# A feed-forward kernel with all five full chunks in seven block products, on ScalarE and VectorE queues written out by hand

## The chip, the cores and the metric

The kernel runs on one NeuronCore of one Trainium2 chip. The metric is the device time of one execution in microseconds (us), the median over the runs shown. TensorE (PE) multiplies matrices into PSUM, VectorE (DVE) and ScalarE (ACT) work elementwise on SBUF and PSUM, GpSimd (POOL) does small work and issues the adding transfers, SyncE (SP) issues the loads.

## The reference, cut to what matters

A trunk of four layers over 256 tokens of width 1024, all in float32. Each layer is a feed-forward block, an attention block (one of three kinds) and a second feed-forward block, so there are eight feed-forward blocks, and only they are changed:

```python
D_FF = 2816
def swiglu(x, w_in, w_out):
    gate, up = jnp.split(x @ w_in, 2, axis=-1)
    return (jax.nn.silu(gate) * up) @ w_out
...
h = h + 0.5 * rms_norm(swiglu(rms_norm(h, g[0]), ffn_w_in[i, 0], ffn_w_out[i, 0]), g[1])
```

## The kernel before, in words

**Precision.** Every product is made of three float32r matmuls: an operand is split into a rounded part `hi` and a rest `lo` (`hilo`, L155 to L157: a copy on ScalarE makes `hi`, then a subtraction on VectorE makes `lo`), and hi·hi, lo·hi and hi·lo are added up in PSUM (`product`, L139). Splitting the weights is most of the work of ScalarE and VectorE.

**Chunks.** A feed-forward block (`ffn`, L282) walks over the 2816 hidden columns in six chunks: five of 512 columns and one of 256. Before, the narrow one stands second: chunk 0 full, chunk 1 narrow, chunks 2 to 5 full. A chunk multiplies both 128-token tiles (t = 0 and 1) by its gate and up weights, applies SiLU and the product, turns the result on TensorE (`turn`) and multiplies it by its rows of `w_out` (`out`), which is done one chunk later (`o(t, k)` inside the next chunk).

**Plain and Winograd chunks.** A chunk in `plain` makes eight block products (two token tiles, two halves of the depth, gate and up) of 12 matmuls each. A full chunk listed in `WINO` goes through `wino` and makes seven, a Strassen-Winograd scheme: the weight quarters are b00, b01 (upper half of the depth, gate and up) and b10, b11 (lower half), and the sums t1 = b00 + b01, t3 = b01 + b11, t2 = t1 + b11 = b00 + t3 and t4 = t2 + b10 (the signs are in the activations and in `nr`). Of these four sums two are additions on VectorE (L372, 128x2048 each) and two are transfers that add while they write, issued by GpSimd (L375). Each of the seven weights is then split.

**Buffers.** A loaded or summed weight lies in one of `RAWS = 9` raw buffers; its split pair lies in one of `UNITS = 4` slots, which `close` frees after the product that reads it. `fill()` issues whatever loads and splits (`preps`, in a fixed order) have room, so the split of unit n + 4 is issued right after the product of unit n. The units of a Winograd chunk are used in the order b00, b10, t2, o0, t1, t3, b11, o2, t4, where o0 and o2 are the two pieces of the chunk before in `w_out`.

**Order of the queues.** A tile framework schedules the traced program: it keeps dependencies, simulates the engines with a cost model, and sorts each engine's instructions by readiness and by the order in which they were written. So the order on ScalarE and VectorE before is the scheduler's. A call of `keep_in_program_order` pins an instruction behind the one traced just before it on the same engine. Once compiled, each engine's list is fixed.

**Where a chunk ends.** After product t4 the gate of tile 1 is closed: VectorE adds (L482), ScalarE applies SiLU (L518), VectorE multiplies (`up`, L426). The next chunk copies its first product to SBUF on ScalarE (`sl0`, L487) before product t2 may be added to the same PSUM bank.

## Time and profile before

| | us |
|---|---|
| median of 3 runs (2003.55 to 2004.16) | 2004.0 |
| profiled execution: its own time | 2004.23 |
| profiled execution: span of the profile | 2002.3 |
| TensorE busy in the span | 1932.5 (97%) |
| VectorE busy | 1609.4 (80%) |
| ScalarE busy | 1257.2 (63%) |

The span runs from the first to the last instruction; 1.9 us of the execution's time lie outside it. Shares are averages over stages that have different limits, so the feed-forward blocks are read by themselves below. The granted TensorE clock was 1.00 (the 2.4 GHz level) in every stretch shown. L numbers are lines of the kernel before.

### The profile page before, as it was taken

Reading aid. Unit: us, or ns where it says so; the run is one execution under the profiler, and the core shown is the slowest. Engines: PE = TensorE matmul, PEld = TensorE weight load, DVE = VectorE, ACT = ScalarE, POOL = GpSimd, SP = SyncE. Lnnn points to the kernel's source line nnn. Section 1 sums busy time; section 2 is a strip of 40 time slices with the busy share of each in tenths; the row PEclk is TensorE's granted clock in tenths of the full one; section 3 lists DMA queues with packets and bytes.
Section 4 is the critical chain, followed back from the end, with each engine's and each line's share of the span. In section 5 each row is a group of like instructions: output and inputs, shape, how many; then the busy total and the mean of one; then the engine's idle time right before and its main releaser. Section 6 shows DMA issues by size and latency. Waiting matters only on the chain.

```text
span 2002.3 us, 25733 instructions
## 1 busy us (share of the span) xinstructions
PE 1932.5 (97%) x9712; PEld 1584.9 (79%) x9712; DVE 1609.4 (80%) x2040; ACT 1257.2 (63%) x1721; POOL 188.6 (9%) x303
## 2 busy tenths in 40 slices
PE   7999999999999999999999999999999999999998
PEld 6777878777877878877887787678778777878776
DVE  6888678888788766788879877877988888678886
ACT  6566666566566566566656666865666657576654
POOL 0001210000000120000000032000000000210000
PEclk9999999999999999999999999999999999999999
DMA  9795638696787556687877675166868785638782
GB/s 360 213 295 140 211 120 294 184 294 188 245 274 222 169 189 212 184 278 211 283 221 212 209 205 165 60 242 200 230 208 300 202 286 148 206 105 286 203 286 55
DMA packets 177867, 430.25 MB, mean 215 GB/s; under 512 B 8784, under 2 KB 37712, under 8 KB 169552
## 3 DMA queue, kind: packets, MB, share of 16 engines
q1 hardware_dynamic: 168528, 361.51, 50.7%
q0 software_dynamic: 9216, 67.11, 17.6%
q8 instruction: 76, 1.25, 0.2%
q14 instruction: 47, 0.39, 0.1%
HBM read 360.43 MB, written 1.05 MB: 181 GB/s over the span
## 4 chain that ended last, share of the span: by engine, by line
PE 79%; ACT 8%; DVE 7%; issue 3%; POOL 0%; ACTq 0%; DVEq 0%; POOLq 0%
PE ps L152 13%; PE pb L152 12%; PE y L246 9%; PE y L244 9%; PE y L245 9%; PE pc L152 6%; ACT hi L156 5%; PE pa L152 4%; PE pw L670 4%; PE pw L672 4%; PE pw L671 3%; DVE lo L157 3%; DVE raw L372 2%; PE tpg L434 1%; ACT gh L156 1%
## 5 line engine op out<-in xcount | busy, mean ns | idle before, releaser
L157 DVE TENSOR_TENSOR lo<-raw,hi 128x2048 fp32r<-128x2048 f32 (+3 forms) x534 | 984.7, 1861 | 251.3 <-ACT hi L156 250.8
L156 ACT CAST hi<-raw 128x2048 fp32r<-128x2048 f32 (+3 forms) x534 | 824.8, 1563 | 481.6 <-DVE raw L372 189.9
L244 PE MATMUL y<-hi,gh 128*128 128x512 f32 x704 | 277.6, 394 | 5.1 <-ACT gh L156 5.1
L245 PE MATMUL y<-lo,gh 128*128 128x512 f32 x704 | 275.2, 391 | 0.0
L246 PE MATMUL y<-hi,gl 128*128 128x512 f32 x704 | 265.7, 391 | 0.0
L152 PE MATMUL ps<-hi,xh 128*128 128x256 f32 (+1 forms) x512 | 175.4, 342 | 1.9 <-ACT xh L156 1.3
L152 PE MATMUL pb<-hi,sh 128*128 128x512 f32 x384 | 153.1, 399 | 21.1 <-ACT sl L487 21.1
L152 PE MATMUL ps<-lo,xh 128*128 128x256 f32 (+1 forms) x512 | 173.2, 338 | 0.2 <-DVE lo L157 0.2
L152 PE MATMUL ps<-hi,xl 128*128 128x256 f32 (+1 forms) x512 | 172.9, 338 | 0.0
L244 PEld LDWEIGHTS y<-hi,gh 128*128 128x128 f32 x704 | 132.2, 188 | 41.7 <-ACT gh L156 15.2
L670 PE MATMUL pw<-hi,xh 128*128 128x512 f32 (+2 forms) x432 | 164.6, 381 | 0.0
L672 PE MATMUL pw<-hi,xl 128*128 128x512 f32 (+2 forms) x432 | 155.9, 361 | 0.0
L671 PE MATMUL pw<-lo,xh 128*128 128x512 f32 (+2 forms) x432 | 155.4, 360 | 0.0
L246 PEld LDWEIGHTS y<-hi,gl 128*128 128x128 f32 x704 | 132.2, 188 | 27.4
L375 POOL DMA_DIRECT2D raw<-raw x64 | 55.5, 868 | 1037.6 <-DVE raw L372 644.3
L245 PEld LDWEIGHTS y<-lo,gh 128*128 128x128 f32 x704 | 132.3, 188 | 26.0
L152 PE MATMUL pb<-lo,sh 128*128 128x512 f32 x384 | 151.8, 395 | 0.0
L152 PE MATMUL pb<-hi,sl 128*128 128x512 f32 x384 | 149.5, 389 | 0.0
L372 DVE TENSOR_TENSOR raw<-raw,raw 128x2048 f32<-128x2048 f32 x64 | 146.0, 2282 | 0.0
L152 PEld LDWEIGHTS ps<-hi,xh 128*128 128x128 f32 x512 | 97.6, 191 | 13.2 <-ACT xh L156 2.2
L152 PEld LDWEIGHTS pb<-hi,sh 128*128 128x128 f32 x384 | 72.0, 188 | 45.3 <-ACT sl L487 31.2
L152 PEld LDWEIGHTS ps<-lo,xh 128*128 128x128 f32 x512 | 97.6, 191 | 11.2 <-DVE lo L157 1.1
(213 smaller groups left out, 3327.2 us busy)
## 6 DMA issues: line engine op xcount, KB each, us to landing
raw<-in_ffn_w_in SPq DMA_DIRECT2D x172, 1024.0 KB, 8.4
raw<-in_ffn_w_out SPq DMA_DIRECT2D x88, 1024.0 KB, 9.2
raw<-raw POOLq DMA_DIRECT2D x64, 1024.0 KB, 7.0
raw<-in_diff_w_in SPq DMA_DIRECT2D x24, 1024.0 KB, 5.2
raw<-in_moba_w_in SPq DMA_DIRECT2D x12, 1024.0 KB, 5.2
raw<-in_nsa_w_in SPq DMA_DIRECT2D x9, 1024.0 KB, 5.1
raw<-in_diff_w_out SPq DMA_DIRECT2D x8, 1024.0 KB, 4.9
gpre<-in_norm_g SPq DMA_DIRECT2D x12, 512.0 KB, 5.9
```

Of the source, the lines that this page charges most:

```text
L152: nc.tensor.matmul(out, l, r, start=first and i == 0, stop=last and i == len(steps) - 1, skip_group_check=more)
L156: self.nc.scalar.copy(hi, src)
L157: self.nc.vector.tensor_tensor(lo, src, hi.bitcast(F32), op=ALU.subtract)
L244: nc.tensor.matmul(y[b], x[0][:, kt, :], hi[:, k, s], start=f, stop=False)
L245: nc.tensor.matmul(y[b], x[0][:, kt, :], lo[:, k, s], start=False, stop=False)
L246: nc.tensor.matmul(y[b], x[1][:, kt, :], hi[:, k, s], start=False, stop=l)
L372: nc.vector.tensor_tensor(R[name(to)], R[name(a)], R[name(b)], op=ALU.add)
L375: nc.gpsimd.dma_start(R[name(to)], R[name(b)], accum_op=ALU.add)
L434: nc.tensor.transpose(tp[:, k, :], g[:, k * P:(k + 1) * P], self.ident)
L670: nc.tensor.matmul(out, x[0][:, kt, :], hi[:, k, :], start=first and i == 0, stop=False)
L671: nc.tensor.matmul(out, x[0][:, kt, :], lo[:, k, :], start=False, stop=False)
L672: nc.tensor.matmul(out, x[1][:, kt, :], hi[:, k, :], start=False, stop=last and i == len(todo) - 1)
```

## The change

- The narrow chunk becomes chunk 0, and all five full chunks (1 to 5) become Winograd chunks.
- The sums of a chunk's weights are ordered otherwise: t1 goes into a raw buffer of its own and t3 = b01 + b11 is added by transfer; both are issued one chunk ahead (`sums_of(j + 1)`, after the first output products of chunk j). t2 = b00 + t3 follows on VectorE when b10 is split, t4 = t2 + b10 by transfer when t2 is split.
- The gate of tile 1 (`gate1`) moves from the end of its chunk to behind the first product and the `sl0` copy of the next, and the `fill()` that stood at the chunk's end goes.
- Inside `wino` every instruction of ScalarE and VectorE is pinned in the order in which it is written (`placed`); TensorE is not.
- The first product of chunk 1 is put in the middle of the narrow chunk, ahead of the turning of tile 1's activations and of their sums (`begin`).

```diff
-WINO = (2, 3, 4, 5)
+WINO = (1, 2, 3, 4, 5)
...
     def hilo(self, src, hi, lo):
-        self.nc.scalar.copy(hi, src)
-        self.nc.vector.tensor_tensor(lo, src, hi.bitcast(F32), op=ALU.subtract)
+        self.placed(self.nc.scalar.copy(hi, src))
+        self.placed(self.nc.vector.tensor_tensor(lo, src, hi.bitcast(F32), op=ALU.subtract))
+    def placed(self, ins):
+        return self.tc.keep_in_program_order(ins) if self.ordered else ins
...
-            chunks.insert(1, (D_FF - 256, 256))
+            chunks.insert(0, (D_FF - 256, 256))
...
             def plan_wino(j):
                 c0, w = chunks[j]
                 name = lambda n: (j, n)
                 quarter = lambda k, u: (w_in, k * 512, 4, u * D_FF + c0, w)
                 c1, w1 = chunks[j - 1]
                 ko = [((j - 1, "o", k), (w_out, c1 + k * P, 2, 0, D)) for k in range(0, w1 // P, 2)]
-                for n, src in ((name("b00"), quarter(0, 0)), (name("b01"), quarter(0, 1)),
-                               (name("b10"), quarter(1, 0)), (name("b11"), quarter(1, 1)), (name("t2"), None), *ko):
+                for n, src in ((name("b00"), quarter(0, 0)), (name("b01"), quarter(0, 1)), (name("b11"), quarter(1, 1)),
+                               (name("t1"), None), (name("b10"), quarter(1, 0)), *ko):
                     loads.append(lambda n=n, src=src: raw(n, src))
-                def add(to, a, b):
-                    nc.vector.tensor_tensor(R[name(to)], R[name(a)], R[name(b)], op=ALU.add)
-                def add_by_dma(to, b):
-                    nc.gpsimd.dma_start(R[name(to)], R[name(b)], accum_op=ALU.add)
-                def quarters(n, then=()):
-                    split(name(n), name(n))
-                    for x in then:
-                        (add if len(x) == 3 else add_by_dma)(*x)
-                def last_of(n, of, gone=None):
-                    split(name(n), name(of), True)
-                    if gone:
-                        free(name(gone))
+                def sum_t2():
+                    split(name("b10"), name("b10"))
+                    self.placed(nc.vector.tensor_tensor(R[name("b00")], R[name("b00")], R[name("b01")], op=ALU.add))
+                def split_t2():
+                    split(name("t2"), name("b00"))
+                    nc.gpsimd.dma_start(R[name("b00")], R[name("b10")], accum_op=ALU.add)
+                def split_t4():
+                    split(name("t4"), name("b00"), True)
+                    free(name("b10"))
                 outs = [lambda n=n: split(n, n, True) for n, _ in ko]
                 preps.extend([
-                    lambda: quarters("b00", [("b00", "b00", "b01")]),
-                    lambda: quarters("b10", [("t2", "b00", "b11"), ("b01", "b11")]),
-                    lambda: quarters("t2", [("t2", "b10")]),
+                    lambda: split(name("b00"), name("b00")),
+                    sum_t2,
+                    split_t2,
                     outs[0],
-                    lambda: last_of("t1", "b00"),
-                    lambda: last_of("t3", "b01"),
-                    lambda: last_of("b11", "b11")])
+                    lambda: split(name("t1"), name("t1"), True),
+                    lambda: split(name("t3"), name("b01"), True),
+                    lambda: split(name("b11"), name("b11"), True)])
                 if j < last:
                     preps.extend(outs[1:])
-                preps.append(lambda: last_of("t4", "t2", "b10"))
+                preps.append(split_t4)
                 if j == last:
                     preps.extend(outs[1:])
+            def sums_of(j):
+                if j not in WINO:
+                    return
+                while (j, "t1") not in R:
+                    loads.pop(0)()
+                b01 = R[j, "b01"]
+                self.placed(nc.vector.tensor_tensor(R[j, "t1"], R[j, "b00"], b01, op=ALU.add))
+                nc.gpsimd.dma_start(b01, R[j, "b11"], accum_op=ALU.add)
             def fill():
...
             def unit(n):
-                fill()
+                if n not in U:
+                    fill()
                 return U[n]
...
             def up(t, src, w, sl, j, r, g=None):
                 if g is None:
                     g = pool.tile([P, 512], F32, tag="g", name=f"g{l}{f}_{j}_{t}")
-                nc.vector.scalar_tensor_tensor(g[:, :w], src[:, :w], r, sl[:, :w], op0=ALU.mult, op1=ALU.mult)
+                self.placed(nc.vector.scalar_tensor_tensor(g[:, :w], src[:, :w], r, sl[:, :w], op0=ALU.mult,
+                                                           op1=ALU.mult))
                 G[j, t] = g
...
                         self.product(ps[:, :w], X[t][0], [(4 * h, unit(n))], h == 0, h == hs[-1])
-                        if i == 1:
-                            self.turn_x()
...
-            def wino(j):
+            def wino(j, gate1):
                 def times(ps, x, at, n, first):
                     self.product(ps, x, [(at, unit((j, n)))], first, True, more=True)
                     close((j, n))
...
                     fill()
                 tile = lambda tag, t: pool.tile([P, 512], F32, tag=tag, name=f"{tag}{l}{f}_{j}_{t}")
-                add = lambda d, x: nc.vector.tensor_tensor(d, x, d, op=ALU.add)
-                s24, s31 = SUMS
+                place = self.placed
+                add = lambda d, x: place(nc.vector.tensor_tensor(d, x, d, op=ALU.add))
                 B = bank("pb")
                 times(B, X[0][0], 0, "b00", True)
-                sl0 = tile("sl", 0)
-                nc.scalar.copy(sl0, B)
+                sl0 = tile("sl", 0) if j > 1 else self.work.tile([P, D], F32, tag="yg", name=f"sl{l}{f}_1_0")[:, :512]
+                place(nc.scalar.copy(sl0, B))
+                gate1()
+                if j == 1:
+                    yield
+                s24, s31 = SUMS
                 fill()
                 turn(j - 1, 0)
                 A = bank("pa")
                 times(A, X[0][0], 4, "b10", True)
                 add(sl0, A)
-                nc.scalar.activation(sl0, sl0, AF.Silu, scale=X[0][1])
+                place(nc.scalar.activation(sl0, sl0, AF.Silu, scale=X[0][1]))
                 fill()
                 turn(j - 1, 1)
                 times(B, s24, 0, "t2", False)
                 sl1 = tile("sl", 1)
-                nc.scalar.copy(sl1, B)
+                place(nc.scalar.copy(sl1, B))
                 fill()
                 o(0, 0)
                 o(1, 0)
+                sums_of(j + 1)
                 times(B, s31, 4, "t1", False)
                 g1 = tile("g", 1)
-                nc.scalar.copy(g1, B)
+                place(nc.scalar.copy(g1, B))
                 fill()
                 C = bank("pc")
                 times(C, s31, 0, "t3", True)
...
                     o(0, 2)
                     o(1, 2)
                 times(C, X[1][0], 4, "t4", False)
-                add(sl1, C)
-                nc.scalar.activation(sl1, sl1, AF.Silu, scale=X[1][1])
-                up(1, g1, 512, sl1, j, nr[1], g1)
-                fill()
+                def gate1():
+                    add(sl1, C)
+                    place(nc.scalar.activation(sl1, sl1, AF.Silu, scale=X[1][1]))
+                    up(1, g1, 512, sl1, j, nr[1], g1)
                 if j < last:
                     del G[j - 1, 0], G[j - 1, 1]
+                yield gate1
             plan_plain(0)
             for j in range(1, last + 1):
...
                     nc.vector.tensor_scalar(r, X[t][1], -1.0, None, op0=ALU.mult)
                     nr.append(r)
-            plain(0, [(0, 0), (1, 0), (0, 1), (1, 1)], [lambda: None, lambda: None, early])
-            zig = [(0, 0), (0, 1), (1, 0), (1, 1)]
+            first = wino(1, lambda: None)
+            sums_of(1)
+            def begin():
+                next(first)
+                self.turn_x()
+                early()
+            plain(0, [(0, 0), (1, 0), (0, 1), (1, 1)], [lambda: None, begin])
             for j in range(1, last + 1):
-                if j in WINO:
-                    wino(j)
-                    continue
-                plain(j, zig, [lambda: turn(j - 1, 0), lambda: turn(j - 1, 1)])
-                for t in range(NT):
-                    out(j - 1, t, (0, 2))
-                for k in (0, 2):
-                    close((j - 1, "o", k))
-                fill()
-                del G[j - 1, 0], G[j - 1, 1]
+                self.ordered = True
+                gate1, = list(first) if j == 1 else wino(j, gate1)
+                self.ordered = False
+            gate1()
+            fill()
             turn(last, 0)
             out(last - 1, 0, (2,))
             ahead()
```

## Rows read from the trace of the kernel before

**Rows 1.** The page: busy time of TensorE; the chain that ended last, by engine.

```profile
PE 1932.5 (97%) x9712; PEld 1584.9 (79%) x9712; DVE 1609.4 (80%) x2040; ACT 1257.2 (63%) x1721; POOL 188.6 (9%) x303
...
PE 79%; ACT 8%; DVE 7%; issue 3%; POOL 0%; ACTq 0%; DVEq 0%; POOLq 0%
```

**Rows 2.** Busy time by stretch: second block whole, its start, chunk 4, its end.

```profile
core 0: us, PE busy (x) PEld busy (x) DVE busy (x) ACT busy (x) POOL busy (x), PEclk, DMA share, GB/s
315.64:499.30 183.66, 178.63 (x853) 147.53 (x853) 155.63 (x128) 115.34 (x115) 10.60 (x13) 1.00 0.77 240
315.64:361.87 46.23, 46.23 (x257) 40.24 (x257) 36.38 (x41) 27.51 (x33) 2.57 (x4) 1.00 0.79 265
421.37:453.95 32.58, 31.47 (x141) 25.43 (x140) 28.70 (x19) 20.21 (x16) 1.71 (x2) 1.00 0.85 258
481.07:499.30 18.23, 18.23 (x89) 15.05 (x88) 16.02 (x24) 11.20 (x21) 2.03 (x2) 1.00 0.86 300
```

**Rows 3.** TensorE's waits: us in total, times, longest us.

```profile
PE pb L152 <- ACT sl L487: 21.1, 24, 0.9
PE tpg L434 <- DVE g L426: 14.1, 8, 1.8
...
PE y L244 <- ACT gh L156: 5.1, 24, 0.2
```

**Rows 4.** Chain of waits in chunk 4, merged: start us, us, what.

```profile
421.53 2.73 PE pb L152 x12
424.26 0.44 PE tpg L434 x4
```

**Rows 5.** Groups by line and shape: busy us, mean ns | idle before.

```profile
L157 DVE TENSOR_TENSOR lo<-raw,hi 128x2048 fp32r<-128x2048 f32 x328 | 745.2, 2286 | 187.7 <-ACT hi L156 187.7
L156 ACT CAST hi<-raw 128x2048 fp32r<-128x2048 f32 x328 | 624.1, 1910 | 426.2 <-DVE raw L372 189.9 <-PE y L246 101.1 <-issue 92.6
...
L372 DVE TENSOR_TENSOR raw<-raw,raw 128x2048 f32<-128x2048 f32 x64 | 146.0, 2282 | 0.0
...
L157 DVE TENSOR_TENSOR gl<-tpg,gh 128x512 fp32r<-128x512 f32 x80 | 54.5, 682 | 0.0
```

**Rows 6.** Instructions that touch the tile sl: ns min/median/max, first and last start.

```profile
L487 ACT COPY sl<-pb x32: 567/575/590, 64.8 to 1957.5; 128x512 f32<-128x512 f32 x32
L482 DVE TENSOR_TENSOR sl<-pa,sl x32: 675/680/682, 69.7 to 1963.1; 128x512 f32<-128x512 f32 x32
...
L518 ACT ACTIVATE sl<-sl,st x32: 712/720/727, 92.4 to 1982.0; 128x512 f32<-128x512 f32 x32
L426 DVE SCALAR_TENSOR_TENSOR g<-g,st,sl x32: 742/746/755, 94.7 to 1982.8; 128x512 f32<-128x512 f32 x32
```

**Rows 7.** VectorE in order of time, chunk 4: start us, us, instruction [idle before].

```profile
421.10 2.28 DVE L372 TENSOR_TENSOR raw<-raw,raw 128x2048 f32<-128x2048 f32 x1
423.30 0.68 DVE L482 TENSOR_TENSOR sl<-pc,sl 128x512 f32<-128x512 f32 x1
425.42 2.29 DVE L157 TENSOR_TENSOR lo<-raw,hi 128x2048 fp32r<-128x2048 f32 x1 [1.44 <-ACT hi L156]
...
428.29 4.49 DVE L157 TENSOR_TENSOR lo<-raw,hi 128x2048 fp32r<-128x2048 f32 x2
432.70 0.68 DVE L157 TENSOR_TENSOR gl<-tpg,gh 128x512 fp32r<-128x512 f32 x1
...
441.41 2.29 DVE L157 TENSOR_TENSOR lo<-raw,hi 128x2048 fp32r<-128x2048 f32 x1 [2.44 <-ACT hi L156]
```

**Rows 8.** ScalarE in order of time, the same chunk.

```profile
423.49 1.90 ACT L156 CAST hi<-raw 128x2048 fp32r<-128x2048 f32 x1 [8.16 <-DVE raw L372]
425.30 0.72 ACT L518 ACTIVATE sl<-sl,st 128x512 f32<-128x512 f32 x1
425.92 1.89 ACT L156 CAST hi<-raw 128x2048 fp32r<-128x2048 f32 x1
```

**Rows 9.** The adding transfers (L375): from issue to landing.

```profile
DMA to landing us min/median/max: 6.9/7.0/9.7
```

More of the change, by code (lines that the diff above doesn't have):

```diff
@@ L540, in early @@
                     nr.append(r)
-            plain(0, [(0, 0), (1, 0), (0, 1), (1, 1)], [lambda: None, lambda: None, early])
-            zig = [(0, 0), (0, 1), (1, 0), (1, 1)]
-            for j in range(1, last + 1):
-                if j in WINO:
-                    wino(j)
-                    continue
-                plain(j, zig, [lambda: turn(j - 1, 0), lambda: turn(j - 1, 1)])
-                for t in range(NT):
-                    out(j - 1, t, (0, 2))
-                for k in (0, 2):
-                    close((j - 1, "o", k))
-                fill()
-                del G[j - 1, 0], G[j - 1, 1]
+            first = wino(1, lambda: None)
[5 more added lines that the diff above has]
+            plain(0, [(0, 0), (1, 0), (0, 1), (1, 1)], [lambda: None, begin])
+            for j in range(1, last + 1):
+                self.ordered = True
+                gate1, = list(first) if j == 1 else wino(j, gate1)
+                self.ordered = False
+            gate1()
+            fill()
             turn(last, 0)
```

## Prediction

> **What bounds the kernel now.** I read the page first. TensorE is busy for 97% of the span and holds 79% of the chain that ended last [rows 1], so at first sight only matmuls count. The change touches the eight feed-forward blocks alone, so I then cut one into stages. The second block takes 183.66 us; its fourth chunk, a Winograd chunk in steady state, takes 32.58 us, and there VectorE is busy for 28.70 us [rows 2]. A product of 12 matmuls costs 2.73 us and four transposes 0.44 us [rows 4]. Such a chunk has 11 products' worth of matmuls (seven, and four for the output of the chunk before) and two groups of transposes: 11 x 2.73 + 2 x 0.44 = 30.9 us. TensorE therefore loses 1.7 us in 32.58, and VectorE has only 3.88 us free. The reader is to see two engines close to their limit, not one. Over all eight blocks TensorE's recorded waits in the chunks are 21.1 us for the `sl0` copy, 14.1 us for the gate that must be turned, 5.1 us for `gh` [rows 3]: 40.3 us in all, 5.0 us a block.
>
> VectorE's own rows show how its time is lost. Two equal splits take 4.49 us and the next instruction starts 4.41 us after the first, so a split or a sum has a pace of 2.20 us although it is recorded with 2.29 (a successor starts 0.08 us before the recorded end) [rows 7]. By that measure additions of 0.68 cost 0.60, multiplications of 0.74 cost 0.66 and `gl` of 0.68 costs 0.60 [rows 5, 6]. A Winograd chunk gives VectorE nine splits, two sums, three additions, two multiplications and two `gl`: 11 x 2.20 + 3 x 0.60 + 2 x 0.66 + 2 x 0.60 = 28.5 us. The rest, 4.1 us, is lost in two places, each time waiting for ScalarE's `hi`: 1.44 and 2.44 us idle [rows 7], 0.08 more each by pace.
>
> **The change, part by part.**
>
> *One more Winograd chunk a block.* It removes one product, 2.73 us of TensorE, in each of eight blocks: 21.8 us. On VectorE it adds three splits, two sums and three additions: 5 x 2.20 + 3 x 0.60 = 12.8 us a block, so that VectorE's 155.63 us [rows 2] become 168.4. ScalarE gets three splits at a pace of 1.81 [rows 8] and three copies of 0.58 [rows 6], 7 us on 115.34 [rows 2], which it has room for. GpSimd issues two more adding transfers of 7.0 us [rows 9]; the chunks keep the DMA engines busy for 0.85 [rows 2], and the longer chunk forecast below lowers that.
>
> *The order on ScalarE and VectorE.* I walk the written order of a chunk 2 to 5 and look for places where two neighbours on VectorE have an instruction of ScalarE between them, because there VectorE cannot run ahead. A handoff costs 0.03 to 0.04 us to `lo` (`hi` starts at 423.49, lasts 1.90, `lo` starts at 425.42) and 0.11 us from a sum to `hi` (421.10 + 2.28 to 423.49) [rows 7, 8]. SiLU of 0.72 gives way to the next `hi` after 0.62 [rows 8].
>
> 1. Sum t2, then `lo` of t2, with `hi` of t2 between: 2.28 + 0.11 + 1.90 + 0.03 = 4.32 us from the sum's start instead of 2.20. Lost: 2.1 us. Before, the addition of the old gate stood in this gap, and the same sum gives 4.32 - 2.20 - 0.60 = 1.52; the row shows 1.44 + 0.08 [rows 7]. So the method holds where it can be tried.
> 2. `gate1`: addition, SiLU, multiplication are neighbours: 0.68 + 0.04 + 0.72 + 0.04 = 1.48 instead of 0.60. Lost: 0.9.
> 3. `hi` of o0 stands behind that SiLU: `lo` of o0 can start 0.72 + 0.62 + 1.90 + 0.03 = 3.27 after the addition's start, the multiplication ends its pace at 1.48 + 0.66 = 2.14. Lost: 1.1.
> 4. The addition to `sl0`, its SiLU, then `hi` of t3, `lo` of t3: 3.27 instead of 0.60. Lost: 2.7. Before, ScalarE did this SiLU after two more splits, and VectorE had no gap there.
> 5. `gl` of tile 1, the last four matmuls of o0 (4 x 2.73 / 12 = 0.91, and by estimate 0.2 until it is seen), `hi` of o2 in the slot that they free: 0.72 + 1.1 + 1.90 + 0.03 = 3.8, against `gl` and one `lo`, 2.8. Lost: 1.0. If TensorE's scheduled order puts other matmuls ahead, up to 1.5 more (before, this gap was 2.5 us).
>
> Together 7.8 us. With 28.5 of work a chunk takes VectorE 36.3 us, over TensorE's 30.9, so it no longer matters which matmuls TensorE does first: VectorE sets the chunk, 3.7 us slower than now.
>
> What hangs on this is that an instruction which waits holds up those behind it. The Trainium skill says so (PSUM — Partial Sum Buffer, Engine vs sequencer instructions): the queues of ScalarE and VectorE are strict FIFO. It speaks against a hand order with close handoffs. The trace agrees as far as it goes, with 1.44 us of VectorE before the split of t2 [rows 7], but shows no case where a ready instruction stood behind. By the rule a chunk is 36.3 us; if waiting instructions could be passed, 28.5 us of VectorE would hide below 30.9.
>
> *`gate1` later and `fill` later.* The removed waits for the `sl0` copy and the gate are TensorE's. They are worth 40.3 us if TensorE sets the pace, and nothing if VectorE does. What is late next is `gh` and `gl`, behind handoffs 3 and 4: TensorE will wait in the output products.
>
> *t1 and t3 a chunk ahead.* From sum t1 to sum t2 VectorE has, in a steady chunk, four splits or sums, an addition and a multiplication: 10.1 us; t3 needs 2.4 + 7.0 = 9.4 us from the same start. It is hidden by 0.7 us. Behind chunk 1 (one output piece, another order) only 7.2 us lie between: 2.2 us wait, from 0 to 4.9 (landing at 9.7 [rows 9]). On GpSimd nothing but the adding transfers is queued inside the chunks, so a late one holds up only the next; on SP a chunk still takes seven raw buffers (t1 has one where t2 had one), so its six loads start as splits free them, as before.
>
> *The start of a block.* Before, VectorE is idle for 46.23 - 36.38 = 9.9 us in the first stage [rows 2]. Now the weights and sums of a Winograd chunk are wanted there, and loads have to land first. The trace has no such start; between 0 and 9.9 us stay idle, and I take the middle, 5. The first product of chunk 1 moved into the narrow chunk covers the turning of tile 1's activations; VectorE has the sums of activations to make at the same time, which is in its busy time already.
>
> **The sum.** VectorE for one block: work 168.4; handoffs 4 and 5 in five chunks 18.5; handoffs 1, 2 and 3 at four borders 16.4; wait for t3 2.2; start 5; end as before, 18.23 - 16.02 = 2.2 [rows 2]. That is 212.7, against 183.66: +29.0 us a block, +232 us in eight. The profiled execution took 2004.23 us, 0.2 above the median of the runs: **2236 us**.
>
> **The rivals.**
>
> - *TensorE keeps setting the pace: faster.* The handoffs are hidden, and the matmuls and waits go: 2004 - 21.8 - 40.3 = 1942 us; if the waits stay, 1982. For it: TensorE's 97% and 79% [rows 1]. Against: it needs the five handoffs together below 30.9 - 28.5 = 2.4 us a chunk, and I count 7.8, of which 6.8 depend on no matmul. Chance 0.08.
> - *The pins change little.* The lists stay about as the scheduler had them, with 4.1 us lost a chunk. Then a block is 168.4 + 5 x 4.1 + 5 + 2.2 + 2.2 = 198.3, +14.6: 2121 us. For it: the pin binds an instruction only to the one traced before it. Against: in `wino` all of them are pinned. Chance 0.07.
> - *Transfers late.* t3 lands after 9.7 us instead of 7.0 in every chunk: 2.0 us more at three borders and 2.7 behind chunk 1, 8.7 a block: 2306 us. For it: sums and loads share the DMA engines. Against: the median is close to the least, 7.0 to 6.9 [rows 9]. Chance 0.05.
> - Between the first two, gains and losses cancel: within 0.2% (4 us, about what a measurement of this kernel can tell). Chance 0.02.
>
> **How the numbers follow.** My forecast has 0.78. Its own range: the start at 0 and no wait for t3 take 7.2 us a block off (2178); the start at 9.9, t3 at 4.9 and a third of handoff 5's 1.5 us in five chunks add 10.1 (2317), but these do not come together; I take 2175 to 2295. The range asked for takes in the late transfers above and reaches a little towards the second rival below: 2150 to 2310, which leaves out 0.17. Faster 0.08, the same 0.02, slower 0.90.
>
> **What would show it.** Right: from one L487 copy to the next in chunks 3 to 5 some 36 us instead of 32.6; VectorE idle about 2.7 us in front of the `lo` behind the `sl0` addition and about 2 us behind sum t2, both ended by ScalarE; VectorE busy about 168 us in a block; TensorE's waits for the `sl0` copy nearly gone, and in their place waits for `gh` and `gl` of some 2 to 4 us in each chunk; TensorE's busy share below 90%. Wrong: chunks of 31 to 33 us, ScalarE's `hi` already done when VectorE comes to it, or a long wait for a raw buffer that is still being added to.

## The result, and the profile after

The changed kernel takes 2310.0 us (median of 4 runs, 2307.7 to 2313.6) against 2004.1 for the kernel before on the same chip: ratio 1.1528, 95% interval 1.1508 to 1.1548. It is slower, as forecast, but by 306 us where I had 232; the median, 2310.02 us, lies just above the upper end of the range, 2310.

L numbers here are those of the changed kernel: `hi` L157, `lo` L158, product L153, output products L249 to L251, sum t2 L379, transfer for t4 L383, sum t1 L411, transfer for t3 L412, multiplication L439, turning L448, additions L495, `sl0` copy L499, its SiLU L509, SiLU of `gate1` L537; in the other runs the same instructions can stand a few lines off. First the page: busy time, and the chain that ended last ("issue" is time for which the profile shows no cause).

```profile
PE 2035.2 (88%) x9616; PEld 1630.7 (71%) x9616; DVE 1719.7 (74%) x2092; ACT 1311.6 (57%) x1757; POOL 196.5 (9%) x319
...
issue 35%; PE 28%; DMA 16%; DVE 13%; ACT 7%; POOL 1%; SPq 0%; POOLq 0%; ACTq 0%; DVEq 0%
```

TensorE fell from 79% of the chain [rows 1] to 28%. VectorE is busy for 110.3 us more than before (8 x 12.8 = 102 forecast), and its idle time, the span of 2311.9 less 1719.7, is 592.2 us against 392.9. The two together are the whole loss, 309.6 us of span. The second block, a stretch in it as long as from one `sl0` copy to the next (461.97 to 500.35), and the sixth block (columns as in [rows 2]):

```profile
361.51:586.16 224.65, 192.39 (x841) 153.30 (x841) 169.84 (x133) 121.96 (x118) 12.39 (x15) 0.92 0.69 206
461.60:500.00 38.40, 33.29 (x141) 26.35 (x140) 29.17 (x18) 20.41 (x17) 1.72 (x2) 0.96 0.74 219
...
1526.57:1743.20 216.63, 188.31 (x842) 150.73 (x841) 167.42 (x129) 121.25 (x116) 10.90 (x13) 0.95 0.67 201
```

VectorE is recorded busy for 29.17 us, about the 28.5 us of work that I had counted for a chunk by pace (the recorded ends lie 0.08 us later, which shows at each of six waits). The chunk takes 38.4 us. What VectorE and TensorE wait for (us in total, times, longest):

```profile
DVE lo L158 <- ACT hi L157: 366.7, 198, 5.6
DVE raw L379 <- DMA raw<-raw: 67.1, 38, 5.1
...
PE y L249 <- ACT gh L157: 62.7, 32, 2.2
...
PE y L251 <- DVE gl L158: 47.5, 33, 1.7
...
PE pb L153 <- ACT sl L499: 1.5, 1, 1.5
```

TensorE's waits for the `sl0` copy, 21.1 us before [rows 3], are down to 1.5; `gh` and `gl` took their place. VectorE in order of time through a chunk shows all five handoffs and the wait for t3 (in brackets the idle time before and what ended it):

```profile
464.31 0.68 DVE L495 TENSOR_TENSOR sl<-pc,sl 128x512 f32<-128x512 f32 x1
465.78 0.75 DVE L439 SCALAR_TENSOR_TENSOR g<-g,st,sl 128x512 f32<-128x512 f32 x1 [0.79 <-ACT sl L537]
467.58 4.49 DVE L158 TENSOR_TENSOR lo<-raw,hi 128x2048 fp32r<-128x2048 f32 x2 [1.05 <-ACT hi L157]
...
472.59 0.68 DVE L495 TENSOR_TENSOR sl<-pa,sl 128x512 f32<-128x512 f32 x1
475.85 2.29 DVE L158 TENSOR_TENSOR lo<-raw,hi 128x2048 fp32r<-128x2048 f32 x1 [2.58 <-ACT hi L157]
478.06 0.68 DVE L158 TENSOR_TENSOR gl<-tpg,gh 128x512 fp32r<-128x512 f32 x1
478.66 2.28 DVE L158 TENSOR_TENSOR lo<-raw,hi 128x2048 fp32r<-128x2048 f32 x1
482.99 2.29 DVE L158 TENSOR_TENSOR lo<-raw,hi 128x2048 fp32r<-128x2048 f32 x1 [2.05 <-ACT hi L157]
485.31 2.29 DVE L411 TENSOR_TENSOR raw<-raw,raw 128x2048 f32<-128x2048 f32 x1
...
496.13 2.29 DVE L379 TENSOR_TENSOR raw<-raw,raw 128x2048 f32<-128x2048 f32 x1 [0.67 <-DMA raw<-raw]
500.48 2.29 DVE L158 TENSOR_TENSOR lo<-raw,hi 128x2048 fp32r<-128x2048 f32 x1 [2.05 <-ACT hi L157]
502.68 0.69 DVE L495 TENSOR_TENSOR sl<-pc,sl 128x512 f32<-128x512 f32 x1
504.16 0.75 DVE L439 SCALAR_TENSOR_TENSOR g<-g,st,sl 128x512 f32<-128x512 f32 x1 [0.79 <-ACT sl L537]
```

From the top: handoff 2 (0.79), 3 (1.05), 4 (2.58), 5 (2.05), the wait for the t3 transfer (0.67), handoff 1 (2.05). TensorE and ScalarE in order of time explain handoff 5, and show what the waits in front of the t2 split hold up:

```profile
478.96 0.63 PE L251 MATMUL y<-hi,gl 128*128 128x512 f32 x2
479.43 0.39 PE L249 MATMUL y<-hi,gh 128*128 128x512 f32 x1
479.66 0.40 PE L250 MATMUL y<-lo,gh 128*128 128x512 f32 x1
479.89 0.39 PE L251 MATMUL y<-hi,gl 128*128 128x512 f32 x1
480.12 0.39 PE L249 MATMUL y<-hi,gh 128*128 128x512 f32 x1
480.35 0.39 PE L250 MATMUL y<-lo,gh 128*128 128x512 f32 x1
480.58 0.39 PE L251 MATMUL y<-hi,gl 128*128 128x512 f32 x1
...
495.08 0.39 PE L153 MATMUL pc<-hi,xl 128*128 128x512 f32 x1
...
481.05 1.91 ACT L157 CAST hi<-raw 128x2048 fp32r<-128x2048 f32 x1 [2.46 <-issue]
```

Handoff 5: behind `gl` (478.06) stand eight matmuls, from 478.96 to 480.97, and `hi` of o2 starts at 481.05, when they are done. (The profile puts this wait down to "issue"; but in three chunks of the sixth block `hi` starts 0.08 us after the eighth too.) I had counted four. And the queue: product t4 into `pc` is done at 495.47 (495.08 + 0.39), yet the addition that reads it starts at 502.68. It stands behind sum t2, which waits for a transfer, and behind `lo` of t2, which waits for `hi`. VectorE is idle for 2.72 (0.67 + 2.05) of those 7.2 us with a ready instruction in its queue. That is the rule that the prediction cited from the Trainium skill (PSUM — Partial Sum Buffer, Engine vs sequencer instructions: ScalarE and VectorE take their queues strictly in order), for which the trace of before had no row; this one agrees.

### The profile page after: what moved, and what is told of

It is laid out like the page before. It is cut to its first block, busy times and chain, and to the rows that moved or that the text cites. A ratio compares the mean times of both kernels' runs of the same rounds, so it can differ in the third digit from the quotient of the medians.

```text
span 2311.9 us, 25631 instructions
## 1 busy us (share of the span) xinstructions
PE 2035.2 (88%) x9616; PEld 1630.7 (71%) x9616; DVE 1719.7 (74%) x2092; ACT 1311.6 (57%) x1757; POOL 196.5 (9%) x319
## 3 DMA queue, kind: packets, MB, share of 16 engines
HBM read 360.43 MB, written 1.05 MB: 156 GB/s over the span
## 4 chain that ended last, share of the span: by engine, by line
issue 35%; PE 28%; DMA 16%; DVE 13%; ACT 7%; POOL 1%; SPq 0%; POOLq 0%; ACTq 0%; DVEq 0%
DMA raw<-raw 10%; DVE lo L158 6%; DMA raw<-in_ffn_w_in 6%; ACT hi L157 5%; PE y L251 4%; PE pb L153 3%; PE y L249 3%; PE y L250 3%; PE pw L692 3%; PE pc L153 3%; PE pw L694 3%; PE pw L693 3%; DVE raw L379 2%; ACT e L777 1%; DVE sl L495 1%
## 5 line engine op out<-in xcount | busy, mean ns | idle before, releaser
L158 DVE TENSOR_TENSOR lo<-raw,hi 128x2048 fp32r<-128x2048 f32 (+3 forms) x546 | 1040.0, 1918 | 367.2 <-ACT hi L157 366.7
L157 ACT CAST hi<-raw 128x2048 fp32r<-128x2048 f32 (+3 forms) x546 | 862.2, 1604 | 542.8 <-DVE raw L379 311.8
L249 PE MATMUL y<-hi,gh 128*128 128x512 f32 x704 | 303.5, 433 | 62.7 <-ACT gh L157 62.7
L251 PE MATMUL y<-hi,gl 128*128 128x512 f32 x704 | 288.4, 433 | 47.6 <-DVE gl L158 47.5
L249 PEld LDWEIGHTS y<-hi,gh 128*128 128x128 f32 x704 | 145.5, 207 | 107.8 <-ACT gh L157 76.1
L153 PE MATMUL pb<-lo,sh 128*128 128x512 f32 x480 | 192.0, 400 | 30.8 <-DVE lo L158 30.8
L251 PEld LDWEIGHTS y<-hi,gl 128*128 128x128 f32 x704 | 142.5, 208 | 93.3 <-DVE gl L158 65.2
L153 PE MATMUL pb<-hi,sh 128*128 128x512 f32 x480 | 191.5, 399 | 13.1 <-ACT sh L157 11.3
L153 PE MATMUL pb<-hi,sl 128*128 128x512 f32 x480 | 192.2, 400 | 7.6 <-DVE sl L158 7.6
L250 PEld LDWEIGHTS y<-lo,gh 128*128 128x128 f32 x704 | 146.1, 207 | 32.3 <-DVE lo L158 2.3
L379 DVE TENSOR_TENSOR raw<-raw,raw 128x2048 f32<-128x2048 f32 x40 | 91.7, 2292 | 67.1 <-DMA raw<-raw 67.1
L153 PEld LDWEIGHTS pb<-lo,sh 128*128 128x128 f32 x480 | 91.8, 191 | 59.7 <-DVE lo L158 41.1
L153 PEld LDWEIGHTS pb<-hi,sh 128*128 128x128 f32 x480 | 92.4, 193 | 37.5 <-ACT sh L157 13.3
L153 PEld LDWEIGHTS pb<-hi,sl 128*128 128x128 f32 x480 | 91.1, 190 | 28.5 <-DVE sl L158 11.5
L509 ACT ACTIVATE sl<-sl,st 128x512 f32<-128x512 f32 x40 | 28.9, 722 | 144.8 <-DVE sl L495 144.8
L412 POOL DMA_DIRECT2D raw<-raw x40 | 34.9, 871 | 758.0 <-DVE raw L411 744.1
L692 PEld LDWEIGHTS pw<-hi,xh 128*128 128x128 f32 x432 | 82.0, 190 | 18.3 <-issue 8.2
L777 ACT ACTIVATE e<-e,st 128x128 f32<-128x128 f32 (+1 forms) x160 | 71.7, 450 | 40.7 <-DVE st L774 39.8
```

The lines of the kernel that those rows point to most:

```text
L153: nc.tensor.matmul(out, l, r, start=first and i == 0, stop=last and i == len(steps) - 1, skip_group_check=more)
L157: self.placed(self.nc.scalar.copy(hi, src))
L158: self.placed(self.nc.vector.tensor_tensor(lo, src, hi.bitcast(F32), op=ALU.subtract))
L249: nc.tensor.matmul(y[b], x[0][:, kt, :], hi[:, k, s], start=f, stop=False)
L250: nc.tensor.matmul(y[b], x[0][:, kt, :], lo[:, k, s], start=False, stop=False)
L251: nc.tensor.matmul(y[b], x[1][:, kt, :], hi[:, k, s], start=False, stop=l)
```

## Experiments

Every kernel is compared with the one before on the same chip (medians 2003.6 to 2004.2 us). "Gaps" are places where VectorE has no instruction between one that ScalarE needs and one that needs ScalarE.

**1. The written order off.** The whole change, but no instruction is pinned.

```diff
-                self.ordered = True
+                self.ordered = False
```

> The changed kernel without a pin: the same chunks, sums and text, but the scheduler sorts ScalarE and VectorE as before. Theory A (close handoffs in the pinned order): most of the loss goes; with the 4.1 us a chunk that VectorE lost before, 2121 us, at most 2170, and VectorE's waits for hi fall from 367 us towards 250. Theory B (the fifth Winograd chunk and the sums by another way load VectorE and the transfers too much, the order is beside the point): 2250 us or more.

Measured: 2084.2 us, ratio 1.0397 (1.0377 to 1.0418), below what either theory gave. So 226 of the 306 us are the price of this written order against the scheduler's; the other 80 are not. In its trace

```profile
DVE lo L158 <- ACT hi L157: 161.3, 129, 5.6
```

VectorE's waits for `hi` fall below those of before (187.7 at the weights alone, [rows 5]).

**2. One gap at a time.** First the SiLU of `sl0` behind the next split (handoff 4):

```diff
-                place(nc.scalar.activation(sl0, sl0, AF.Silu, scale=X[0][1]))
                 fill()
+                place(nc.scalar.activation(sl0, sl0, AF.Silu, scale=X[0][1]))
```

> Only handoff 4 is taken away: the SiLU of sl0 is written behind the split that followed it. Theory A: 2.58 us in each of five chunks of eight blocks, 103 us, so about 2207 us (2195 to 2230), and VectorE's wait in front of the lo behind the sl0 addition is gone. Theory B, or TensorE's waits and its clock setting the pace: 2290 us or more.

Then the sums of the next chunk between the two o products (into handoff 5):

```diff
                 o(0, 0)
-                o(1, 0)
                 sums_of(j + 1)
+                o(1, 0)
```

> Only the place of sum t1 changes: between the two output products of o0 instead of behind them, so that on VectorE it stands in the gap before the split of o2 (handoff 5) and the transfer of t3 starts earlier. Theory A with the two terms that the forecast had too small: 2.05 us or more in four chunks and the waits of sum t2 for the transfer (67 us over the kernel) go, 65 to 67 us each, so 2180 us (2170 to 2245). If handoff 5 is not VectorE's gap but TensorE's output products waiting, no change.

Then the same, but with the t3 transfer still written behind o(1, 0):

```diff
-                nc.gpsimd.dma_start(b01, R[j, "b11"], accum_op=ALU.add)
+                if j == 1:
+                    nc.gpsimd.dma_start(b01, R[j, "b11"], accum_op=ALU.add)
...
                 o(0, 0)
+                sums_of(j + 1)
                 o(1, 0)
-                sums_of(j + 1)
+                if (j + 1, "b01") in R:
+                    nc.gpsimd.dma_start(R[j + 1, "b01"], R[j + 1, "b11"], accum_op=ALU.add)
```

> The changed kernel with the VectorE addition for t1 alone moved between the two o products (where it fills the wait for the split of o2); the transfer for t3 is issued where it was, behind them. Theory A (my forecast went wrong mostly at that handoff, 11.9 us a block where I had 5.0; it holds seven matmuls, not four): about 9.5 us a block come back, 2310 - 76 = 2234 us, 2220 to 2250. Theory B (what the earlier run with both moved gave back, 95 us, was the wait for t3, 6.9 us a block where I had 2.2): 2265 us or more.

Measured: 2247.7 us (1.1213, 1.1190 to 1.1235), 2214.7 (1.1048, 1.1026 to 1.1070) and 2215.9 (1.1058, 1.1038 to 1.1078). VectorE's idle rows in the sixth block, added up by kind, us (each row is of the kind shown above):

| | changed | SiLU moved | t1 and t3 moved |
|---|---|---|---|
| handoff 1 | 7.5 | 7.5 | 7.5 |
| handoffs 2 and 3 | 7.3 | 7.3 | 7.3 |
| handoff 4 | 12.9 | 3.8 | 12.9 |
| handoff 5 | 11.9 | 9.5 | 2.1 |
| wait for t3 | 6.9 | 8.9 | 4.0 |
| all idle rows of VectorE | 48.9 | 39.5 | 36.3 |

Moving the SiLU gave back 62 us, not 103, a time between the ranges of the two theories: 0.76 us a chunk stay in handoff 4, and a chunk that is faster reaches its t2 sum earlier, so the wait for t3 grows by 2.0 us a block. Moving the sums gave back 95 us, within what was expected, where handoff 5 and the wait for t3 at the forecast's sizes would allow 58 (8 x 7.2) if both went whole. The third kernel told nothing apart, and its time lies outside both ranges: in both kernels GpSimd issued the transfer about 0.4 us (median) after the end of the t1 sum. (Where its expectation says seven matmuls, the trace has the eight shown above.) That handoff 5 is the larger part (9.8 of 12.6 us) rests on the idle rows, not on a run of its own.

**3. All five gaps filled, the pins kept.** The SiLU moved as above, and these (`gate1(0)` is the addition, `gate1(1)` SiLU and multiplication):

```diff
-                gate1()
                 if j == 1:
                     yield
+                else:
+                    gate1(0)
                 s24, s31 = SUMS
                 fill()
+                if j > 1:
+                    gate1(1)
...
-                    split(name("b10"), name("b10"))
                     self.placed(nc.vector.tensor_tensor(R[name("b00")], R[name("b00")], R[name("b01")], op=ALU.add))
+                    split(name("b10"), name("b10"))
...
                 turn(j - 1, 1)
+                sums_of(j + 1)
                 times(B, s24, 0, "t2", False)
...
                 o(1, 0)
-                sums_of(j + 1)
```

> Pins stay, all five handoffs are filled by another order: SiLU of sl0 behind the next split, sum t1 ahead of product t2, sum t2 ahead of the split of b10, and the addition of gate1 ahead of two splits with its SiLU and multiplication behind them. Theory A: VectorE's 28.5 us a chunk fit below TensorE's 30.9, so the block is TensorE's again with one product less and few waits: 1990 us (1960 to 2050), faster than before or equal. Theory B: the work and the transfers are the limit, so 2150 us or more.

Measured: 2060.0 us (1.0279, 1.0261 to 1.0296), 10 above the range expected, but 250 less than the changed kernel with the same instructions and the same pins. So it is not pinning that costs these 250 us, but what stands next to what. Its windows: the start of the fifth block, the whole sixth block, a steady chunk; and under them TensorE and VectorE in order of time in the start of the fifth block (L378 is sum t2 there).

```profile
1010.72:1045.00 34.28, 26.21 (x155) 23.44 (x154) 27.91 (x33) 19.49 (x28) 5.21 (x5) 0.90 0.82 257
...
1366.01:1548.99 182.98, 176.33 (x841) 145.46 (x840) 166.97 (x130) 122.52 (x117) 11.60 (x13) 1.00 0.78 239
1442.77:1474.97 32.20, 31.33 (x143) 25.54 (x141) 29.34 (x19) 20.65 (x17) 1.71 (x2) 1.00 0.85 261
```

```profile
1027.57 0.55 PE L153 MATMUL ps<-hi,xh 128*128 128x256 f32 x1 [7.08 <-DVE g L439]
...
1022.46 2.29 DVE L378 TENSOR_TENSOR raw<-raw,raw 128x2048 f32<-128x2048 f32 x1 [4.41 <-DMA raw<-raw]
```

The steady chunk is back at 32.2 us (38.4 in the changed kernel, 32.58 before) with TensorE busy for 31.3. What is left sits in the starts: VectorE stands 4.41 us at chunk 1's t2 sum until its t3 transfer has landed, TensorE 7.08 us. The table gives, from first matmul to first matmul of the next block, what each kernel takes beyond before, in us (odd blocks with the attention behind them):

| block | 1 | 2 | 3 | 4 | 5 | 6 | 7 |
|---|---|---|---|---|---|---|---|
| changed | 46.5 | 41.0 | 38.6 | 32.3 | 39.3 | 33.3 | 37.7 |
| order off | 21.7 | 12.7 | 7.4 | 5.3 | 6.0 | 5.8 | 9.3 |
| gaps filled | 12.8 | 9.7 | 8.2 | -0.5 | 7.1 | -0.4 | 7.5 |

With gaps filled two blocks lose nothing and the others 7 to 13 us. What differs is when chunk 1's sums come: its t1 sum, and with it the t3 transfer, starts 11.6 us ahead of the block's first matmul in blocks 4 and 6, where sum t2 then waits for nothing, but 2.3 us ahead of it in blocks 3, 5 and 7 and 6.3 us behind it in blocks 2 and 8, where sum t2 waits 4.4 to 5.2 us.

**4. Chunk 1's t3 on VectorE,** in the kernel with gaps filled.

```diff
-                nc.gpsimd.dma_start(b01, R[j, "b11"], accum_op=ALU.add)
+                if j == 1:
+                    nc.vector.tensor_tensor(b01, b01, R[j, "b11"], op=ALU.add)
+                else:
+                    nc.gpsimd.dma_start(b01, R[j, "b11"], accum_op=ALU.add)
```

> The kernel with all five gaps filled (2060.0 us), with one edit: for chunk 1 alone the sum for t3 is an addition of VectorE (2.28 us), not a transfer issued by GpSimd. Theory A (what is left over before, 56 us, is lost at the starts of six of the eight blocks, where VectorE stands 4.4 to 5.9 us at the sum for t2 until chunk 1's t3 transfer has landed, and TensorE behind it): the wait goes and 2.3 us of work come in its place: about 3 us a block and a little more where TensorE waited too, 2036 us, 2025 to 2050. Theory B (the narrow chunk is simply too short to cover the preparation of chunk 1, whoever adds): 2060 within 8 us, or more.

Measured: 2038.9 us (1.0179, 1.0163 to 1.0194), as theory A had it. The transfer is 21 of the 56 us. Blocks 4 and 6, which had not waited, lose 4.4 and 3.1 us by the added work.

**5. The narrow chunk second again, four chunks in seven products.** The new sums and the later `gate1` stay; `sums_of(2)` is issued ahead of the narrow chunk's products, and the early first product of chunk 1 (`begin`) goes. The two lines that set this:

```diff
-WINO = (1, 2, 3, 4, 5)
+WINO = (2, 3, 4, 5)
...
-            chunks.insert(0, (D_FF - 256, 256))
+            chunks.insert(1, (D_FF - 256, 256))
```

A first try of the three kernels had the sums of chunk 2 behind the narrow chunk's products. There t2 is taken before b01 has become t3, so it is another sum, and these kernels compute something else: their times (2288.2 us pinned, 2112.7 unpinned, 2116.2 with gaps filled) say nothing here. With the sums ahead:

> Four chunks in seven products again, the narrow chunk second, the written order kept; the sums of chunk 2 now stand ahead of the narrow chunk's products, so that they come before that chunk's first preparation (in the three kernels before, the t2 sum of chunk 2 was taken too early and is another sum). Theory A (the written order costs about 6 us in each chunk, wherever the narrow chunk stands): 2004 + 8 x 26 = 2212 us, 2170 to 2260. Theory B (narrow chunk first and fifth chunk are what costs): at most 2080 us.

> The same without the written order: of the change only the order of the sums is left, with a transfer for t3 in place of a VectorE addition. Theory A (the sums alone cost nothing, the 80 us of the unpinned five-chunk kernel sit at the block starts): 2004 us, 1985 to 2025. Theory B (each chunk pays for its second transfer, which lands in 11 us in the unpinned five-chunk kernel and 7.0 before): 2040 us or more.

> Four chunks, narrow one second, the written order with all five gaps filled. Theory A (the steady chunk takes 32.2 us with gaps filled against 32.6 before, and the block start is that of before): 1990 us, 1975 to 2015, so not slower than before. Theory B (pins or sums keep a cost of their own): 2030 us or more.

Measured: pinned 2188.8 us (1.0921, 1.0899 to 1.0943), unpinned 2026.2 (1.0109, 1.0092 to 1.0125), gaps filled 2007.8 (1.0016, 1.0007 to 1.0026). The gaps cost 181 us in 32 chunks here and 250 in 40 there: 5.7 and 6.3 us a chunk, wherever the narrow chunk stands. The new sums (with the later `gate1`) cost 22 us in the scheduler's order, just above theory A's range. There, once a block, VectorE waits at chunk 3's t2 sum for its t3 transfer (L379, in the second block), and TensorE behind it for that unit's `hi`:

```profile
PE pb L153 <- ACT hi L157: 19.0, 8, 4.1
```

```profile
397.42 2.29 DVE L379 TENSOR_TENSOR raw<-raw,raw 128x2048 f32<-128x2048 f32 x1 [4.18 <-DMA raw<-raw]
```

With gaps filled 3.6 us are left (0.16%): not faster, as theory A's 1990 would have been, and hardly slower. The narrow chunk first, the fifth chunk and `begin` together cost 2060.0 - 2007.8 = 52 us, though they take 21.8 us of work off TensorE.

**6. Is there a version that beats both?** In the four-chunk kernel with gaps filled TensorE waits, in a steady chunk, only for the turned gate. Next, the gate behind one split instead of two (`fill(1)` issues at most one); then also the second split behind the turn. Both edits were run in the five-chunk kernel of experiment 4 as well, with its t3 of chunk 1 a transfer again in blocks 4 and 6.

```diff
-                fill()
+                fill(1)
                 if j > 1:
                     gate1(1)
+                fill()
                 turn(j - 1, 0)
```

> Four chunks, narrow one second, gaps filled (2007.8 us, same as before within 0.2%), with one edit: the SiLU and the multiplication for the gate of tile 1 stand behind one split, not behind two. In its trace TensorE's only recorded wait in a steady chunk is 0.87 us for that gate to be turned. Theory A (TensorE sets the pace there): 0.87 us in three to four chunks of eight blocks, 20 to 28 us: 1984 us, 1975 to 1995, faster than before. Theory B (another wait of VectorE or of a transfer comes in its place): 2000 to 2010 us.

> Five chunks, narrow one first, gaps filled, the t3 sum of chunk 1 on VectorE (2038.9 us) but a transfer in the two blocks that lost by that (3 us each), and the gate behind one split. Theory A: 4 x 0.87 us in eight blocks, 28 us, and 7 us for the two blocks: 2004 us, 1992 to 2020. Theory B (the starts, not the steady chunks, hold what is left): 2025 us or more.

```diff
                 if j > 1:
                     gate1(1)
-                fill()
                 turn(j - 1, 0)
+                fill()
```

> The four-chunk kernel with gaps filled and the gate behind one split (2007.4 us), with the second split moved behind the turning of tile 0's gate. In that kernel TensorE's wait of 0.87 us for the turned gate had given way to one of 0.98 us for gl, which stood on VectorE behind that split (2.2 us). Theory A (this is the last close wait of the steady chunk): 0.98 us in three chunks of eight blocks, 24 us: 1984 us, 1972 to 1996. Theory B (the next instruction of the same chain is late instead): 2000 to 2010 us.

> The same edit on the five-chunk kernel (2034.7 us). Theory A: 0.98 us in four chunks of eight blocks, 31 us: 2003 us, 1990 to 2015. Theory B: the next wait of the chain takes its place: 2025 us or more.

Measured: four chunks 2007.4 us (1.0017, 1.0008 to 1.0026), then 2001.7 (0.9987, 0.9978 to 0.9996); five chunks 2034.7 (1.0155, 1.0141 to 1.0169), then 2026.0 (1.0109, 1.0095 to 1.0122). Each lies in theory B's range, the last by 1 us; the five-chunk kernel gained 4 and 9 us of the 35 and 31 that theory A allowed. TensorE in order of time, at its wait in a steady chunk, in the four-chunk kernel with gaps filled, then after the first edit, then after the second:

```profile
1451.29 0.33 PE L448 MATMUL tpg<-ident,g 128*128 128x128 f32 x1 [0.86 <-DVE g L439]
```

```profile
1447.71 0.50 PE L251 MATMUL y<-hi,gl 128*128 128x512 f32 x1 [0.98 <-DVE gl L158]
```

```profile
1447.88 0.50 PE L249 MATMUL y<-hi,gh 128*128 128x512 f32 x1 [0.77 <-ACT gh L157]
```

One wait goes and the next instruction of the chain (multiplication, turn, `gh`, `gl`) is late instead: TensorE's waits for this chain are 39.1 us in all, then 40.8, then 37.0. Of these 22.0 and 22.6 us in the last two are a longer wait once a block, 2.3 to 3.8 us, that neither edit touched. VectorE stands at chunk 3's t2 sum (L378) until its t3 transfer has landed, and the multiplication (L440) that TensorE's turn waits for stands behind that sum. In the sixth block of the last kernel:

```profile
1400.44 2.29 DVE L378 TENSOR_TENSOR raw<-raw,raw 128x2048 f32<-128x2048 f32 x1 [3.21 <-DMA raw<-raw]
```

```profile
1405.65 0.66 PE L449 MATMUL tpg<-ident,g 128*128 128x128 f32 x4 [2.85 <-DVE g L440]
```

In all eight blocks TensorE's wait is 0.35 us shorter than VectorE's. It comes to more than what the two edits went after, and no run took it away. 2001.7 us is below both kernels, but only by 0.13% against the kernel before (0.04 to 0.22), and the single times overlap (1998.0 to 2003.8, and 2001.7 to 2006.0): hardly a gain.

## Why the prediction was right in kind and too low

- *VectorE sets the chunk: right.* Chunks take 38.4 us and VectorE has 28.5 of work in them; with gaps filled, and nothing else done, they take 32.2. The signs named came too: 2.58 us idle in front of the `lo` behind the `sl0` addition, 2.05 behind sum t2, TensorE busy for 88%, and its waits for `gh` and `gl`, 2.16 and 1.65 us in the chunk shown.
- *VectorE's work: right.* 168.4 us a block forecast, 167.4 in the sixth block, 169.8 in the second.
- *Handoffs 1 to 4: right.* Per block, with 0.08 us of pace for each as in the forecast: 1 to 3 together 15.8 us (16.4), handoff 4 13.3 (13.5).
- *Handoff 5: the term that failed.* The step was "the last four matmuls of o0". TensorE's list had done only the first four of that output product when `gl` came, so eight stood behind it: 2.0 us instead of 0.9. Measured 2.05 to 3.3 us idle, 12.3 us a block with the pace, where I had 5.0: 7.3 us a block more. The four extra matmuls are about 5.5 of these (5 x 1.1); 1.6 more come from two chunks in which TensorE itself was late (one is shown in the last section). I had written down up to 1.5 more a chunk, 7.5 a block, if TensorE's order put other matmuls ahead, and then let only a third of it into the range.
- *The wait for t3: mis-sized.* I took the landing of before, 7.0 us, a median over t3 and t4 transfers together [rows 9], and let the issue follow the t1 sum after 0.1 us. In the changed kernel the t3 transfers are issued 0.4 us behind the sum (median) and take 8.2:

```profile
DMA to landing us min/median/max: 7.2/8.2/11.7
```

  So what I called hidden by 0.7 us waits, in the sixth block, 0.7 to 1.3 in steady chunks and 4.1 behind chunk 1: 6.9 us a block for 2.2, or 4.7 more. It was my third rival in part.
- *The start of a block: right on average only.* I took 5 us; in the sixth block VectorE is idle for 0.2 there. But the sixth block loses 33.3 us and the average block 38.7 (309.6 / 8), and with gaps filled all that is left of such differences lies in the starts. If it does here too (not shown), a start costs 0.2 + 5.4 = 5.6 us on average. The trace shows 2.4 of it: chunk 1's own t2 sum waits for its t3 transfer, 1.0 to 5.1 us in six blocks and not at all in blocks 4 and 6.
- *The sum.* Against +29.0 us a block: handoff 5 +7.3, t3 +4.7, start +0.6, work -1.0, handoffs 1 to 4 -0.8, together +10.8, or 86 us in eight blocks. The span missed by 309.6 - 232 = 78; the sixth block does not stand for all to the last us. The first two terms are the miss.
- *The range.* I narrowed its upper end because "these do not come together". Two of them did: handoff 5 took nearly the whole of its 1.5 us a chunk, and the wait for t3 came to 6.9 us a block where I had let in 4.9.
- *The rivals.* TensorE did not keep pace. "The pins change little" was wrong, but the kernel without pins took 2084 us where I had put 2121 for it.

Left open: why chunk 1's sums come so early in blocks 4 and 6 that these lose nothing at their start with gaps filled, while block 2, with attention ahead of it too, loses 9.7; what the four-chunk kernel would take without the 22 us at chunk 3's t2 sum; and whether the five-chunk kernel's 22 us can be had with a start that loads and adds chunk 1 sooner. That was not tried beyond experiments 4 and 6.

## What to carry to other kernels

A queue written by hand costs what stands between neighbours: for each pair on one engine with an instruction of another engine between them, count the gap, and put ready work into it; the same instructions and pins took 2310 and 2060 us. A handoff that passes through TensorE is sized by the matmuls that its list still holds at that moment, not by those that depend on the operand alone. And where two engines are both near their limit, removing a wait of the one shows the next instruction of the same chain: 0.86, 0.98, 0.77 us. Look at the rare long waits too, not at the steady stretch alone: 2.3 to 3.8 us once a block came to 22 us.

## What the hardware showed that I had not expected

TensorE is busy for 103 us more than before, though it has 21.8 us less to do. Parts of its matmuls run at the lower clock: the mean granted clock of the profiled execution is 0.946, and 0.998 before. By estimate that is 2311.9 x 0.054 - 2002.3 x 0.002 = 121 us of lost clock, about the 125 that have to be explained. In the chunk shown above TensorE waits three times within ten microseconds, and by the end of the third wait its clock has fallen. The waits, and windows ahead of the third, behind it and later (the eighth figure is the granted clock):

```profile
464.44 0.50 PE L153 MATMUL pb<-lo,sh 128*128 128x512 f32 x1 [1.30 <-DVE lo L158]
...
469.88 0.50 PE L249 MATMUL y<-hi,gh 128*128 128x512 f32 x1 [2.16 <-ACT gh L157]
...
472.73 1.22 PE L251 MATMUL y<-hi,gl 128*128 128x512 f32 x2 [1.65 <-DVE gl L158]
```

```profile
467.00:471.00 4.00, 1.84 (x10) 1.07 (x8) 3.42 (x2) 2.82 (x3) 0.00 (x0) 1.00 0.97 197
472.73:476.00 3.27, 3.27 (x8) 2.59 (x9) 0.69 (x2) 2.69 (x3) 0.00 (x0) 0.51 0.93 273
477.00:481.00 4.00, 4.00 (x19) 3.29 (x18) 3.94 (x3) 1.59 (x1) 0.00 (x0) 1.00 1.05 395
```

The clock is 1.00 (2.4 GHz), then 0.51 (1.2 GHz) for 3.3 us, then 1.00 again. Where VectorE sets the chunk this need not cost time (not shown), but it can. In the fourth Winograd chunk of the sixth block TensorE runs at the lower clock up to 1673.98, and the eight matmuls of handoff 5 start at 1675.39, 1.5 us after the end of `gl`, where it was 0.2 us in the chunk above; VectorE is idle for 3.33 us there instead of 2.05:

```profile
1667.86:1673.98 6.12, 6.12 (x14) 4.74 (x15) 3.54 (x4) 5.28 (x5) 0.00 (x0) 0.50 0.97 339
```

```profile
1673.19 0.68 DVE L158 TENSOR_TENSOR gl<-tpg,gh 128x512 fp32r<-128x512 f32 x1
...
1675.39 0.62 PE L251 MATMUL y<-hi,gl 128*128 128x512 f32 x2
...
1679.40 2.29 DVE L158 TENSOR_TENSOR lo<-raw,hi 128x2048 fp32r<-128x2048 f32 x1 [3.33 <-ACT hi L157]
```

With all gaps filled the mean granted clock is 0.984, and TensorE is busy for 1932.8 us, as long as before the change, with 21.8 us less to do.

The t3 transfers, too, land later in the faster kernel: 8.2 us in the changed kernel, where a steady chunk moves 219 GB/s, and with gaps filled, at 261 GB/s,

```profile
DMA to landing us min/median/max: 8.2/10.9/12.8
```

The t4 transfers, of the same size, take 7.1 and 7.3 us (median) in the same two kernels, so the higher rate alone does not explain it; what runs beside a t3 transfer was not taken apart. A transfer that is hidden in a slow version need not be hidden in a faster one.
